# Experts' weights loaded as pairs of chunks into fixed places, with ACT and DVE held to the program's order, in a two-block transformer kernel

## The chip, the cores and the metric

One core of a Trainium2 chip runs the whole program. The metric is the device time of one execution in microseconds (us). Engines: PE multiplies matrices (PEld is its weight load), DVE, ACT and POOL work elementwise, SP issues the loads.

## The reference

All is float32 on 256 tokens of width 1024. The first block holds a retention layer, a dense gated layer, a band-attention layer and a mixture of experts; the second holds two hybrid layers and their MLPs. What the change touches is the mixture of experts:

```
def swiglu(x, w_gate, w_up, w_down):
    return (jax.nn.silu(x @ w_gate) * (x @ w_up)) @ w_down

def moe_swiglu(xn, w_router, w_gate, w_up, w_down):
    logits = (xn @ w_router).astype(jnp.float32)
    top_v, top_i = lax.top_k(logits, TOP_K)
    top_w = jax.nn.softmax(top_v, axis=-1)
    gates = jnp.sum(jax.nn.one_hot(top_i, N_EXPERTS, dtype=jnp.float32) * top_w[..., None], axis=-2)
    gates = gates.astype(xn.dtype)
    y = jnp.zeros_like(xn)
    for e in range(N_EXPERTS):
        y = y + gates[..., e:e + 1] * swiglu(xn, w_gate[e], w_up[e], w_down[e])
    return y
```

Each expert has an inner width of 3584, so its three matrices are 14 x 3 MB of float32.

## The kernel before

**Split products.** PE multiplies in a shorter float format (fp32r). So each float32 operand is split into a high part (ACT copies it into that format) and a low part (DVE subtracts the high part from the original), and a product is three matmuls: high by high, low by high, high by low (`mm3`, L341).

**The stream of weights.** The weights lie in DRAM in the order of use, packed by `packed` (L168) into chunks of 1 MB, 128 partitions by 2048 floats. `Stream` (L228) moves them. `fill` (L256) issues a load on SP's queue into a buffer `wraw` as soon as a pool has a free one: 4 in the pool "raw", and from the attention layer until the last expert's last chunk 3 and 4 more (`widen`, L249), 11 MB in all. `_split` (L277) splits a chunk as two parts of 128x1024: ACT writes `whi` (L288), DVE `wlo` (L289). The last expert's parts are split as two halves of 128x512. `get` (L297) hands the parts to the matmuls and keeps the splits 5 parts ahead, as many as the pool of split parts has buffers.

**The experts.** `experts` (L997) takes the eight experts in turn. Five are *wide* (first, third, fourth, sixth, seventh): room for 128 tokens, three matmuls a product. Three are *narrow* (second, fifth, eighth): room for 64 tokens, whose high and low halves lie side by side, two matmuls a product. An expert has 14 steps. A step has the up product (two chunks, so four parts, here called A, B, C, D; 24 matmuls of 128x512 wide, 16 narrow) and the down product of the step before (one chunk, parts E and F; 12 or 8 matmuls). A prime marks a part of the next step, two primes of the one after that. What is between them:

- wide: sg (ACT's Silu L1031, DVE's product L1032), two transposes on PE (tp, L1038), and the split of tp into hh (ACT, L348) and hl (DVE, L349), which the down product reads;
- narrow: cp (ACT copies the sums, L1043), the fold on PE (tp, L1048, which transposes and adds the halves; 4 matmuls, 8 passes in the trace), sgn (ACT L1052, DVE L1053), and the split of sgn into the two halves of hh (ACT L348, DVE L349).

At the end of an expert the result goes through yh and yl to the tokens' places (L1091, L1093), and for the next pair of experts the tokens are gathered (L956). The `tc.If(most > P)` branch at the end of `moe_layer` doesn't run on these inputs.

**What sets the order.** The program issues instructions in the order of the Python code; the framework's scheduler then orders each engine's instructions by priority and its own estimate of when operands are ready, and each engine works through its list in that order, waiting at semaphores. In the code, `split()` of a step is called after `w.get` of the next step's first up chunk, so after all splits that this call makes.

Of the kernel before, what the change touches and what calls it, by code (L numbers as in the profile page):

```python
# [11 lines left out]
F32 = mybir.dt.float32  # L12
# [3 lines left out]
AF = mybir.ActivationFunctionType  # L16
ALU = mybir.AluOpType
# [150 lines left out]
def packed(plan, arrays):  # L168
    offs, total = offsets(plan)
    out = np.empty(max(total, 1), np.float32)  # L170
    for c, o in zip(plan, offs):
        dst = out[o:o + P * c.kt * c.n].reshape(P, c.kt, c.n)
# [55 lines left out]
class Stream:  # L228


    def __init__(self, prog, plans, raw_bufs, hl_bufs, raw_pool, hl_pool):
        self.nc = prog.nc
        self.items, self.parts, self.first = [], [], []
        for ap, plan in plans:
            offs, _ = offsets(plan)
            for c, o in zip(plan, offs):
                self.first.append(len(self.parts))
                step = max(c.kt // 2, 1)
                self.parts += [(len(self.items), k, step) for k in range(0, c.kt, step)]
                self.items.append((ap, c, o))  # L240
        self.expert = prog.expert
        self.first.append(len(self.parts))
        self.free = {raw_pool: raw_bufs}
        self.base, self.extra = raw_pool, []
# [4 lines left out]
    def widen(self, pool, bufs, until):  # L249

        self.extra.append(pool)
        self.free[pool] = bufs
        self.last = next(i for i, it in enumerate(self.items) if it[1].key == until)
        self.fill()

    def fill(self, most=None):  # L256
        while self.n_raw < min(len(self.items), most or len(self.items)):
            pool = next((p for p in self.extra if self.n_raw <= self.last and self.free[p]), self.base)
            if not self.free[pool]:
                return  # L260
            ap, c, o = self.items[self.n_raw]
            f = c.kt * c.n
            t = pool.tile([P, 2048], F32, name="wraw")
            if c.key[0] in ("eu", "ed"):
                e = self.expert[c.key[1]] if c.key[1] else 0
                src = ap[e:e + 1] if isinstance(e, int) else ap[bass.ds(e, 1)]
                self.nc.sync.dma_start(t[:, :f], src[:, o:o + P * f].rearrange("o (p f) -> (o p) f", p=P))
            else:
                step = f if self.n_raw else f // 2
                for c0 in range(0, f, step):  # L270
                    self.nc.sync.dma_start(t[:, c0:c0 + step],
                                           bass.AP(tensor=ap.tensor, offset=ap.offset + o + c0, ap=[[f, P], [1, step]]))
            self.free[pool] -= 1
            self.raw[self.n_raw] = t, pool
            self.n_raw += 1

    def _split(self):  # L277
        i, k, nk = self.parts[self.n_hl]
        c = self.items[i][1]
        self.fill()  # L280
        t, pool = self.raw[i]
        f = nk * c.n
        hi, lo = (self.hl_pool.tile([P, 1024], F32R, name=n) for n in ("whi", "wlo"))
        n = 1 if c.key[0] in ("eu", "ed") and c.key[1] < NE - 1 else 2
        for i0 in range(0, f, f // n):
            h, l = (x[:, i0:i0 + f // n] for x in (hi, lo))
            src = t[:, k * c.n + i0:k * c.n + i0 + f // n]
            self.nc.scalar.activation(h, src, AF.Copy)  # L288
            self.nc.vector.tensor_tensor(l, src, h.bitcast(F32), op=ALU.subtract)  # L289
        if k + nk == c.kt:  # L290
            self.free[pool] += 1
            del self.raw[i]
        self.hl[self.n_hl] = [x[:, :f].rearrange("p (k n) -> p k n", n=c.n) for x in (hi, lo)]
        self.n_hl += 1
        self.fill()

    def get(self, *keys):  # L297

        at = self.first[self.n_get]
        for key in keys:  # L300
            assert self.items[self.n_get][1].key == key, (self.items[self.n_get][1].key, key)
            self.n_get += 1
        end = self.first[self.n_get]
        while self.n_hl < min(max(end, at + self.hl_bufs), len(self.parts)):
            self._split()
        return [[x[:, k, :] for x in self.hl[i]] for i in range(at, end) for k in range(self.parts[i][2])]


class Program:
    RAW, HL = 4, 5  # L310

    def __init__(self, tc, io, stop=None, dump=None):
        self.tc, self.nc, self.io = tc, tc.nc, io
        self.stop, self.dump_ap = stop, dump
        self.fence, self.in_set = [], []
        self.turns = {}
        self.expert = {}
# [28 lines left out]

    def split_psum(self, hi, lo, ps):
        self.nc.scalar.activation(hi, ps, AF.Copy)  # L348
        self.nc.vector.tensor_tensor(lo, ps, hi.bitcast(F32), op=ALU.subtract)  # L349

# [137 lines left out]
    def run(self):  # L488
        nc, io = self.nc, self.io
        self.we = io["we"].rearrange("(e f) -> e f", e=NE)  # L490
        with ExitStack() as st, ExitStack() as self.later, \
                ExitStack() as self.routed, ExitStack() as self.wide:
            pool = self.lasting = lambda *a, **kw: st.enter_context(self.pool(*a, **kw))
            raw_pool, hl_pool = pool("raw", self.RAW), pool("hl", self.HL)
            self.keep, self.gains = pool("keep", 1), pool("gains", 1)
# [285 lines left out]

    def widen(self, name, bufs):

        self.w.widen(self.wide.enter_context(self.pool(name, bufs)), bufs, ("ed", NE - 1, FFE // 256 - 1))

    def attention_layer(self):
# [3 lines left out]
        with self.pool("bando", side="right") as outs, ExitStack() as mid, ExitStack() as first:  # L790
# [206 lines left out]
    def experts(self, px, pool, gates, slot, w, first, wide):  # L997
# [5 lines left out]
        for e in range(NE):  # L1003
# [21 lines left out]
            def turned(j, ps):  # L1025
# [3 lines left out]
                if wide[e]:  # L1029
                    sg = self.work.tile([P, 256], F32, name="sg", tag="xs", bufs=3)  # L1030
                    nc.scalar.activation(sg, ps[:, :256], AF.Silu)  # L1031
                    nc.vector.tensor_tensor(sg, sg, ps[:, 256:], op=ALU.mult)  # L1032
                    hT[j] = (hh, pool.tile([P, 2, P], F32R, name="hl", bufs=2))

                    def turn():
                        tp = self.bank("tp")
                        for k in range(2):
                            nc.tensor.transpose(tp[:, k * P:(k + 1) * P], sg[:, k * P:(k + 1) * P], self.ident)  # L1038
                        return lambda: self.split_psum(*hT[j], tp[:, :256].rearrange("p (k s) -> p k s", k=2))
# [3 lines left out]
                nc.scalar.activation(cp, ps, AF.Copy)  # L1043

                def turn():
# [3 lines left out]

                    def split():  # L1050
                        sg = self.work.tile([P, 2, 64], F32, name="sgn", tag="xs", bufs=3)
                        nc.scalar.activation(sg, tp[:, :2], AF.Silu)  # L1052
                        nc.vector.tensor_tensor(sg, sg, tp[:, 2:], op=ALU.mult)  # L1053
                        self.split_psum(hh[:, :, :64], hh[:, :, 64:], sg)
                    return split
                return turn

            split = None
            for j in range(nj):
                ps = self.bank("mm")  # L1060
                for k0 in (0, 4):
                    wu = w.get(("eu", e, j, k0 * P))
                    if split:
                        split()
                        split = None
                    for k in range(4):
# [3 lines left out]
                if j == nj - 1:  # L1070
# [4 lines left out]
                    down(rows[:2])  # L1075
                    turn()()
                    down(rows[2:], True)
                else:
                    turn = turned(j, ps)
                    down(rows)  # L1080
                    split = turn()
            with self.tc.high_priority(offset=300) if e == NE - 1 else nullcontext():
# [12 lines left out]
    def moe_layer(self):  # L1095
        nc, tc, io = self.nc, self.tc, self.io
        with self.pool("moex") as px, self.pool("moe") as pool:
            with self.banks(acc="67", mm="45", tp="01", ps="23"):
# [14 lines left out]
                self.experts(px, pool, gates, slot, self.w, first, WIDE)  # L1113
        self.wide.close()
        with tc.If(most > P):
            with self.pool("moe2") as pool, self.pool("raw2", 2) as raw, \
# [4 lines left out]
                self.experts(pool, pool, gates, slot, again, self.gather(pool, pool, slot, GROUPS[0], wide), wide)  # L1121
        self.routed.close()
        return self.at("e")
# [488 lines left out]
```

## Time and profile before

| what | us |
|---|---|
| runs before | 2430.64, 2432.98, 2434.96; median 2432.98 |
| the profiled execution's own time | 2430.28 |
| its span | 2428.5 |
| PE busy | 2369.9 (98 %) |
| DVE busy | 1892.6 (78 %) |
| ACT busy | 1567.7 (65 %) |
| wlo on DVE (L289), 1656 instructions | 1383.4 |
| whi on ACT (L288), 1656 instructions | 1204.1 |
| expert stage, from the first expert's first product to the last's end | 568 to 1532 |

The span runs from the first to the last instruction; the execution's own time has a little around it. "Busy" counts an engine's instructions, not its waits; matmuls are pipelined, so that one shows 0.39 us while the next starts 0.23 us after it. The eight experts begin at about 568, 694, 805, 935, 1056, 1174, 1293 and 1420 us. Of the 606 MB that the program loads, 336 loads of 1 MB are the experts'; in the expert stage the 16 DMA engines are 83 to 97 % busy by expert, against 30 to 70 % in most of the rest. A row of waits names an engine and line, what it waited for, the total, the count and the longest. In a timeline, `x4` is four instructions one behind the other under one start and one duration, and the bracket at a row's end is the engine's idle time before it with what ended it.

### The profile page before, as it was taken

The numbers are of one execution on the slowest core, as the hardware profiler recorded it, in microseconds if no ns is written. First come the engines' busy times: TensorE is split into PE (matmuls) and PEld (weight loads), VectorE is DVE, ScalarE is ACT, GpSimd is POOL, SyncE is SP. The second block draws the span as 40 slices with busy tenths as digits, with TensorE's granted clock in tenths as the row PEclk, the third lists the DMA queues.
The fourth block names the chain that finished last, engine by engine and source line by source line (L and its number), as shares of the span: only waits on it lengthen the run. The fifth ranks groups of instructions, "written<-read, shape, count | busy, mean of one in ns | idle before, by whom it ended". The sixth has DMA issues, their size and how long they took to land. (4 is left out here: it accounts for less than half of the span.)

```text
span 2428.5 us, 35659 instructions
## 1 busy us (share of the span) xinstructions
PE 2369.9 (98%) x13032; PEld 1972.4 (81%) x13032; DVE 1892.6 (78%) x3026; ACT 1567.7 (65%) x2609; POOL 61.1 (3%) x105
## 2 busy tenths in 40 slices
PE   8999999999999999999999999899999999999999
PEld 6978998887876787876788876698789989878998
DVE  6756567778999889899998899878776567877655
ACT  6446555667888777778777789645755554575554
POOL 0000000000000000000000000100000000100000
PEclk9999999999999999999999999999999999999999
DMA  7445555567989998999999999534345554434553
GB/s 286 167 174 208 191 191 191 194 247 265 369 333 394 360 359 335 359 356 409 356 369 343 364 356 393 148 132 161 133 167 199 189 173 139 170 126 177 194 189 107
DMA packets 88393, 605.72 MB, mean 249 GB/s; under 512 B 10480, under 2 KB 12144, under 8 KB 17296
## 3 DMA queue, kind: packets, MB, share of 16 engines
q1 hardware_dynamic: 85792, 593.91, 65.4%
q0 software_dynamic: 2416, 9.44, 1.7%
q8 instruction: 104, 1.70, 0.3%
q14 instruction: 81, 0.66, 0.1%
HBM read 602.26 MB, written 1.05 MB: 248 GB/s over the span
## 5 line engine op out<-in xcount | busy, mean ns | idle before, releaser
L289 DVE TENSOR_TENSOR wlo<-wraw,whi 128x512 fp32r<-128x512 f32 (+1 forms) x1656 | 1383.4, 876 | 369.4 <-ACT whi L288 356.1
L288 ACT ACTIVATE whi<-wraw 128x512 fp32r<-128x512 f32 (+1 forms) x1656 | 1204.1, 776 | 438.9 <-PE mm L344 201.9
L343 PE MATMUL mm<-xth,whi 128*128 128x256 f32 x1296 | 366.3, 283 | 0.0
L345 PE MATMUL mm<-xth,wlo 128*128 128x256 f32 x1296 | 364.0, 281 | 1.2 <-DVE wlo L289 1.2
L344 PE MATMUL mm<-xtl,whi 128*128 128x256 f32 x1296 | 364.2, 281 | 0.0
L345 PEld LDWEIGHTS mm<-xth,wlo 128*128 128x128 f32 x1296 | 247.1, 191 | 2.1 <-DVE wlo L289 1.4
L343 PEld LDWEIGHTS mm<-xth,whi 128*128 128x128 f32 x1296 | 243.6, 188 | 4.9 <-issue 3.0
L344 PEld LDWEIGHTS mm<-xtl,whi 128*128 128x128 f32 x1296 | 243.8, 188 | 3.7 <-issue 2.1
L344 PE MATMUL acc<-wlo,hh 128*128 128x512 f32 x624 | 243.6, 390 | 0.0
L345 PE MATMUL acc<-whi,hl 128*128 128x512 f32 x624 | 243.5, 391 | 0.0
L343 PE MATMUL acc<-whi,hh 128*128 128x512 f32 x624 | 231.6, 391 | 1.5 <-ACT hh L348 1.5
L343 PE MATMUL mm<-whi,xth 128*128 128x512 f32 (+2 forms) x592 | 231.7, 391 | 0.6 <-ACT whi L288 0.4
L344 PE MATMUL mm<-wlo,xth 128*128 128x512 f32 (+2 forms) x592 | 231.5, 391 | 0.3 <-DVE wlo L289 0.3
L345 PE MATMUL mm<-whi,xtl 128*128 128x512 f32 (+2 forms) x592 | 229.5, 388 | 0.5 <-DVE xtl L349 0.5
L343 PE MATMUL mm<-whi,xgh 128*128 128x512 f32 x560 | 226.2, 404 | 2.6 <-ACT whi L288 2.6
L344 PE MATMUL mm<-wlo,xgh 128*128 128x512 f32 x560 | 223.8, 400 | 3.0 <-DVE wlo L289 3.0
L345 PE MATMUL mm<-whi,xgl 128*128 128x512 f32 x560 | 222.2, 397 | 0.0
L1013 PE MATMUL mm<-wlo,xgh 128*128 128x512 f32 x336 | 143.2, 426 | 5.2 <-DVE wlo L289 4.4
L343 PEld LDWEIGHTS acc<-whi,hh 128*128 128x128 f32 x624 | 117.1, 188 | 26.4 <-ACT hh L348 3.3
L345 PEld LDWEIGHTS acc<-whi,hl 128*128 128x128 f32 x624 | 117.1, 188 | 25.0 <-DVE hl L349 0.6
L344 PEld LDWEIGHTS acc<-wlo,hh 128*128 128x128 f32 x624 | 117.2, 188 | 23.4 <-DVE wlo L289 0.3
L1012 PE MATMUL mm<-whi,xgh 128*128 128x512 f32 x336 | 134.4, 400 | 0.0
(386 smaller groups left out, 3091.7 us busy)
## 6 DMA issues: line engine op xcount, KB each, us to landing
wraw<-in_we_dram SPq DMA_DIRECT2D x336, 1024.0 KB, 5.8
wraw<-in_w_dram SPq DMA_DIRECT2D x218, 1024.0 KB, 4.8
wraw<-in_w_dram SPq DMA_DIRECT2D x4, 912.0 KB, 4.7
wraw<-in_w_dram SPq DMA_DIRECT2D x6, 512.0 KB, 3.6
bias<-in_rel_rows_dram POOLq DMA_DIRECT2D x4, 768.0 KB, 4.6
gain<-in_norm_ffn_dram POOLq DMA_DIRECT2D x2, 512.0 KB, 6.6
gn<-in_ret_gn_dram SPq DMA_DIRECT2D x4, 256.0 KB, 3.2
gain<-in_norm_ple_dram POOLq DMA_DIRECT2D x2, 512.0 KB, 6.6
```

What stands on the lines that cost most here:

```text
L288: self.nc.scalar.activation(h, src, AF.Copy)
L289: self.nc.vector.tensor_tensor(l, src, h.bitcast(F32), op=ALU.subtract)
L343: mm(out, l[0], r[0], start=start, stop=False)
L344: mm(out, l[0], r[1], start=False, stop=False)
L345: mm(out, l[1], r[0], start=False, stop=stop)
L1012: nc.tensor.matmul(out, x[0], wk[0], start=start, stop=False)
L1013: nc.tensor.matmul(out, x[0], wk[1], start=False, stop=stop)
```

## The change

1. `packed` lays two neighbouring chunks of an expert side by side for each partition, and `fill` loads such a pair with one DMA of 2 MB into two neighbouring places of a fixed tile. The places are tiles of 4, 2 and 4 chunks (10 MB) in the place of pools of 4, 3 and 4 buffers (11 MB). A place is free when both its parts are split; a pair is loaded when two neighbouring places are free.
2. `inorder` chains instructions of ACT, and of DVE, so that the scheduler keeps them in the program's order: the experts' whi and wlo, sg, cp, sgn, hh and hl.
3. `get` takes steps to put `between` its splits: hh and hl of a wide step stand behind the first split that the call makes; of a narrow step, sgn behind the first and hh behind the second.

```diff
 def packed(plan, arrays):
...
+        if c.key[0] in ("eu", "ed"):
+            o -= half * P * c.kt * c.n
+            dst = out[o:o + 2 * P * c.kt * c.n].reshape(P, 2, c.kt, c.n)[:, half]
+            half = 1 - half
...
+    def room(self, pool, n, last):
+        t = pool.tile([P, n, 2048], F32, name="wraw")
+        self.last[id(t)] = last
+        self.free += [(t, k) for k in range(n)]
...
     def fill(self, most=None):
         while self.n_raw < min(len(self.items), most or len(self.items)):
-            pool = next((p for p in self.extra if self.n_raw <= self.last and self.free[p]), self.base)
-            if not self.free[pool]:
+            ap, c, o, n = self.items[self.n_raw]
+            free = [p for p in self.free if self.n_raw < self.last[id(p[0])]]
+            size = 1
+            if n is not None and self.pairs:
+                assert n % 2 == 0
+                size = 2
+                free = [(t, k) for t, k in free if k % 2 == 0 and (t, k + 1) in self.free]
+            if not free:
                 return
...
-                self.nc.sync.dma_start(t[:, :f], src[:, o:o + P * f].rearrange("o (p f) -> (o p) f", p=P))
+                src = src[:, n // 2 * 2 * P * f:(n // 2 + 1) * 2 * P * f].rearrange("o (p k f) -> (o p) k f", p=P, k=2)
+                self.nc.sync.dma_start(t[:, k:k + size], src[:, n % 2:n % 2 + size])
...
     def _split(self):
...
-            self.nc.scalar.activation(h, src, AF.Copy)
-            self.nc.vector.tensor_tensor(l, src, h.bitcast(F32), op=ALU.subtract)
+            act = self.nc.scalar.activation(h, src, AF.Copy)
+            dve = self.nc.vector.tensor_tensor(l, src, h.bitcast(F32), op=ALU.subtract)
+            if c.key[0] in ("eu", "ed"):
+                self.prog.inorder(act=act, dve=dve)
...
-    def get(self, *keys):
+    def get(self, *keys, between=()):
...
         while self.n_hl < min(max(end, at + self.hl_bufs), len(self.parts)):
             self._split()
+            if between:
+                between.pop(0)()
+        for step in between:
+            step()
...
+    def inorder(self, **ins):
+        for e, i in ins.items():
+            self.after(i, [self.line[e]] if e in self.line else [])
+            self.line[e] = i
...
-            self.widen("raw3", 3)
+            self.widen("raw3", 2)
...
             for j in range(nj):
                 ps = self.bank("mm")
                 for k0 in (0, 4):
-                    wu = w.get(("eu", e, j, k0 * P))
-                    if split:
-                        split()
-                        split = None
+                    wu = w.get(("eu", e, j, k0 * P), between=steps)
+                    steps = []
```

The rest of the diff passes `sg`, `cp`, `sgn`, `hh` and `hl` through `inorder` and returns the steps of `turn` as a list. `self.after` adds an order without a semaphore. Outside the expert stage every engine's instructions stay in their order.

How the order moves in three places (L1066, L1078, L1088, L307, L375 and L1073 of the change are L1031, L1043, L1052, L288, L348 and L1038 of before). ACT, a step in the middle of the third expert (wide), before:

```order
L1031 ACTIVATE sg<-mm 128x256
L288 ACTIVATE whi<-wraw 128x1024 x2
L348 ACTIVATE hh<-tp 128x256
L288 ACTIVATE whi<-wraw 128x1024 x4
L1031 ACTIVATE sg<-mm 128x256
```

and of the change:

```order
L1066 ACTIVATE sg<-mm 128x256
L307 ACTIVATE whi<-wraw 128x1024
L375 ACTIVATE hh<-tp 128x256
L307 ACTIVATE whi<-wraw 128x1024 x5
L1066 ACTIVATE sg<-mm 128x256
```

hh has moved ahead of one split; five splits stand behind it, not four. PE in the same expert where the transposes (tp) of a step in the middle stand, before, with the tiles' numbers (acc are the down product's sums, mm the next up product's):

```order
L344 MATMUL acc_8210<-wlo_8916,hh_8870 128x512
L345 MATMUL acc_8210<-whi_8915,hl_8874 128x512
L1038 MATMUL tp_8964<-ident_83,sg_8948 128x128 x2
L343 MATMUL mm_8967<-whi_8921,xgh_7106 128x512
L344 MATMUL mm_8967<-wlo_8922,xgh_7106 128x512
```

and of the change, a step in the middle of the same expert:

```order
L371 MATMUL mm_8695<-wlo_8667,xgh_6943 128x512
L372 MATMUL mm_8695<-whi_8666,xgl_6944 128x512
L370 MATMUL mm_8695<-whi_8671,xgh_6943 128x512
L371 MATMUL mm_8695<-wlo_8672,xgh_6943 128x512
L372 MATMUL mm_8695<-whi_8671,xgl_6944 128x512
L1073 MATMUL tp_8692<-ident_84,sg_8676 128x128 x2
L370 MATMUL mm_8695<-whi_8671,xgh_6943 128x512
L371 MATMUL mm_8695<-wlo_8672,xgh_6943 128x512
```

The transposes stood right behind the down matmuls; they now stand behind 15 of the next step's 24 up matmuls (part whi_8671 is the third of its four), in the next step behind 13, and so on by turns. ACT, a step in the middle of the fifth expert (narrow), before:

```order
L1043 ACTIVATE cp<-mm 128x512
L288 ACTIVATE whi<-wraw 128x1024 x2
L1052 ACTIVATE sgn<-tp 128x128
L288 ACTIVATE whi<-wraw 128x1024 x2
L348 ACTIVATE hh<-sgn 128x2x64
L288 ACTIVATE whi<-wraw 128x1024 x2
L1043 ACTIVATE cp<-mm 128x512
```

and of the change:

```order
L1078 ACTIVATE cp<-mm 128x512
L307 ACTIVATE whi<-wraw 128x1024
L1088 ACTIVATE sgn<-tp 128x128
L307 ACTIVATE whi<-wraw 128x1024
L375 ACTIVATE hh<-sgn 128x2x64
L307 ACTIVATE whi<-wraw 128x1024 x4
L1078 ACTIVATE cp<-mm 128x512
```

sgn and hh stand one split earlier each, four splits follow. On PE the fold, which stood between the down matmuls, now stands behind 9 and 6 by turns of the next step's 16 up matmuls (in the last expert behind 11 and 10).

## Rows read from the trace of the kernel before

**Rows 1.** Windows, fifth expert: us; PE, PEld, DVE, ACT, POOL busy; clock; DMA share; GB/s.
```profile
1056.00:1174.00 118.00, 111.48 (x508) 80.18 (x507) 113.21 (x128) 101.50 (x137) 0.00 (x0) 1.00 0.97 387
```

**Rows 2.** Waits of ACT in the expert stage, 568 to 1540 us: total, times, longest.
```profile
ACT whi L288 <- DMA wraw<-in_we_dram: 7.8, 23, 0.8
```

**Rows 3.** Waits of SP's queue, 607 to 1500 us: total, times, longest.
```profile
SPq L267 <- DVE wlo L289: 466.1, 201, 6.6
```

**Rows 4.** The experts' loads as one tile: from issue to landing.
```profile
DMA to landing us min/median/max: 4.6/5.8/11.7
```

**Rows 5.** Timeline of PE in a wide step: start, duration, instruction, idle before.
```profile
975.85 0.38 PE L1038 MATMUL tp<-ident,sg 128*128 128x128 f32 x2
...
976.30 0.39 PE L344 MATMUL mm<-wlo,xgh 128*128 128x512 f32 x1
...
981.42 0.40 PE L345 MATMUL mm<-whi,xgl 128*128 128x512 f32 x1
...
984.38 0.38 PE L1038 MATMUL tp<-ident,sg 128*128 128x128 f32 x2
```

**Rows 6.** Timeline of ACT in the same wide step.
```profile
976.26 0.39 ACT L348 ACTIVATE hh<-tp 128x256 fp32r<-128x256 f32 x1 [0.66 <-PE tp L1038]
976.61 3.90 ACT L288 ACTIVATE whi<-wraw 128x1024 fp32r<-128x1024 f32 x4
```

**Rows 7.** Timeline of DVE in the same wide step.
```profile
977.70 4.63 DVE L289 TENSOR_TENSOR wlo<-wraw,whi 128x1024 fp32r<-128x1024 f32 x4 [0.32 <-ACT whi L288]
```

**Rows 8.** Timeline of ACT in a narrow step of the fifth expert.
```profile
1089.02 0.28 ACT L1052 ACTIVATE sgn<-tp 128x128 f32<-128x128 f32 x1 [0.36 <-PE tp L1048]
1089.19 2.00 ACT L288 ACTIVATE whi<-wraw 128x1024 fp32r<-128x1024 f32 x2
...
1096.56 0.28 ACT L1052 ACTIVATE sgn<-tp 128x128 f32<-128x128 f32 x1 [0.37 <-PE tp L1048]
```

**Rows 9.** Timeline of DVE in the same narrow step.
```profile
1092.55 0.28 DVE L349 TENSOR_TENSOR hh<-sgn,hh 128x128 fp32r<-128x128 f32 x1
1092.75 2.35 DVE L289 TENSOR_TENSOR wlo<-wraw,whi 128x1024 fp32r<-128x1024 f32 x2
```

**Rows 10.** Timeline of PE in the last expert.
```profile
1471.79 1.00 PE L1048 MATMUL tp<-fold,cp 128*128 128x64 f32 x8
```

**Rows 11.** Timeline of ACT in the last expert.
```profile
1461.60 0.61 ACT L288 ACTIVATE whi<-wraw 128x512 fp32r<-128x512 f32 x1
...
1465.21 0.28 ACT L1052 ACTIVATE sgn<-tp 128x128 f32<-128x128 f32 x1 [0.18 <-PE tp L1048]
...
1472.83 0.28 ACT L1052 ACTIVATE sgn<-tp 128x128 f32<-128x128 f32 x1 [0.18 <-PE tp L1048]
```

**Rows 12.** Timeline of DVE in the last expert.
```profile
1466.89 2.50 DVE L289 TENSOR_TENSOR wlo<-wraw,whi 128x512 fp32r<-128x512 f32 x4
...
1469.50 4.91 DVE L289 TENSOR_TENSOR wlo<-wraw,whi 128x512 fp32r<-128x512 f32 x8
```

**Rows 13.** Timeline of ACT, early steps of the second expert (narrow).
```profile
704.07 0.58 ACT L1043 ACTIVATE cp<-mm 128x512 f32<-128x512 f32 x1
...
766.91 0.60 ACT L1043 ACTIVATE cp<-mm 128x512 f32<-128x512 f32 x1 [0.84 <-PE mm L1013]
```

**Rows 14.** Timeline of ACT, first step of the fifth expert.
```profile
1070.21 0.60 ACT L1043 ACTIVATE cp<-mm 128x512 f32<-128x512 f32 x1 [1.99 <-PE mm L1013]
...
1078.69 0.60 ACT L1043 ACTIVATE cp<-mm 128x512 f32<-128x512 f32 x1 [1.18 <-PE mm L1013]
```

**Rows 15.** Waits of PE where the second expert ends, 798 to 808 us.
```profile
PE mm L343 <- ACT whi L288: 1.3, 1, 1.3
PE mm L344 <- DVE wlo L289: 0.8, 1, 0.8
```

**Rows 16.** Busy time and granted clock there.
```profile
804.00:806.00 2.00, 2.00 (x6) 1.57 (x5) 1.53 (x2) 0.60 (x1) 0.00 (x0) 0.50 1.02 430
```

**Rows 17.** Waits of PE where the fifth expert ends, 1163 to 1180 us.
```profile
PE mm L343 <- ACT whi L288: 1.2, 1, 1.2
```

More of the change, by code (lines that the diff above doesn't have):

```diff
@@ L170, in packed @@
     out = np.empty(max(total, 1), np.float32)
+    half = 0
     for c, o in zip(plan, offs):
-        dst = out[o:o + P * c.kt * c.n].reshape(P, c.kt, c.n)
+        if c.key[0] in ("eu", "ed"):
+            o -= half * P * c.kt * c.n
+            dst = out[o:o + 2 * P * c.kt * c.n].reshape(P, 2, c.kt, c.n)[:, half]
+            half = 1 - half
+        else:
+            dst = out[o:o + P * c.kt * c.n].reshape(P, c.kt, c.n)
         at = 0
@@ L239, in __init__ @@
                 self.parts += [(len(self.items), k, step) for k in range(0, c.kt, step)]
-                self.items.append((ap, c, o))
+                self.items.append((ap, c, o, plan.index(c) if c.key[0] in ("eu", "ed") else None))
         self.expert = prog.expert
         self.first.append(len(self.parts))
-        self.free = {raw_pool: raw_bufs}
-        self.base, self.extra = raw_pool, []
+        self.free, self.last = [], {}
+        self.room(raw_pool, raw_bufs, len(self.items))
         self.hl_pool, self.hl_bufs = hl_pool, hl_bufs
@@ L247, in __init__, with widen @@
         self.n_raw = self.n_hl = self.n_get = 0
[L249 to L253, printed above, removed]
+    def room(self, pool, n, last):
+        t = pool.tile([P, n, 2048], F32, name="wraw")
+        self.last[id(t)] = last
+        self.free += [(t, k) for k in range(n)]
+    def widen(self, pool, n, until):
+        self.room(pool, n, 1 + next(i for i, it in enumerate(self.items) if it[1].key == until))
         self.fill()
@@ L270, in fill @@
                 for c0 in range(0, f, step):
-                    self.nc.sync.dma_start(t[:, c0:c0 + step],
+                    self.nc.sync.dma_start(t[:, k, c0:c0 + step],
                                            bass.AP(tensor=ap.tensor, offset=ap.offset + o + c0, ap=[[f, P], [1, step]]))
-            self.free[pool] -= 1
-            self.raw[self.n_raw] = t, pool
-            self.n_raw += 1
+            for i in range(size):
+                self.free.remove((t, k + i))
+                self.raw[self.n_raw] = t, k + i
+                self.n_raw += 1
     def _split(self):
@@ L295, in _split @@
         self.fill()
-    def get(self, *keys):
+    def get(self, *keys, between=()):
+        between = list(between)
         at = self.first[self.n_get]
@@ L315, in __init__ @@
         self.fence, self.in_set = [], []
-        self.turns = {}
+        self.turns, self.line = {}, {}
         self.expert = {}
@@ L780, in softmax_pair, with widen @@
         self.split_psum(*out, po[:, :T])
-    def widen(self, name, bufs):
-        self.w.widen(self.wide.enter_context(self.pool(name, bufs)), bufs, ("ed", NE - 1, FFE // 256 - 1))
+    def widen(self, name, n):
+        self.w.widen(self.wide.enter_context(self.pool(name)), n, ("ed", NE - 1, FFE // 256 - 1))
     def attention_layer(self):
@@ L1048, in turn, with silu @@
                         nc.tensor.matmul(tp[:, c], cp[:, c * P:(c + 1) * P], self.fold, start=True, stop=True)
[L1050 to L1055, printed above, removed]
+                    sg = self.work.tile([P, 2, 64], F32, name="sgn", tag="xs", bufs=3)
+                    def silu():
+                        self.inorder(act=nc.scalar.activation(sg, tp[:, :2], AF.Silu),
+                                     dve=nc.vector.tensor_tensor(sg, sg, tp[:, 2:], op=ALU.mult))
+                    return [silu, lambda: self.split_psum(hh[:, :, :64], hh[:, :, 64:], sg, True)]
                 return turn
-            split = None
+            steps = []
             for j in range(nj):
@@ L1061, in experts @@
                 for k0 in (0, 4):
-                    wu = w.get(("eu", e, j, k0 * P))
-                    if split:
-                        split()
-                        split = None
+                    wu = w.get(("eu", e, j, k0 * P), between=steps)
+                    steps = []
                     for k in range(4):
@@ L1075, in experts @@
                     down(rows[:2])
-                    turn()()
+                    for step in turn():
+                        step()
                     down(rows[2:], True)
@@ L1080, in experts @@
                     down(rows)
-                    split = turn()
+                    steps = turn()
             with self.tc.high_priority(offset=300) if e == NE - 1 else nullcontext():
@@ L1114, in moe_layer @@
         self.wide.close()
+        self.line = {}
         with tc.If(most > P):
-            with self.pool("moe2") as pool, self.pool("raw2", 2) as raw, \
+            with self.pool("moe2") as pool, self.pool("raw2") as raw, \
                     self.pool("hl2", 4) as hl, self.banks(acc="67", mm="45", tp="01", ps="23"):
```

32 lines of the change are left out of this document (17 added, 15 removed).

## The prediction, made before the change was run

> **What bounds the kernel now.** I went first to the waits of the loads, since the change is named after them. SP's queue waits mostly for DVE's wlo [rows 3]: a load goes out when its place has been split, not when the memory is ready. ACT, the first reader of a load, waited for one 23 times in the whole expert stage, 7.8 us together [rows 2]. So loads do not bound it, and 7.8 us is the most that faster ones could give.
>
> Then the windows and timelines, step by step. In a **wide** expert PE is the bound: from transpose to transpose 8.53 us [rows 5], the matmuls one behind the other at 0.23 us (22 from 976.30 to 981.42). In a **narrow** one DVE is: it is busy 113.21 of 118 us [rows 1], and a step lasts 7.54 us (sgn at 1089.02, then 1096.56) [rows 8]. In the last expert, whose splits are halves, it lasts 7.62 us (1465.21 to 1472.83) [rows 11]. ACT has idle time in both, but it is in the middle of every chain: what stands behind what on ACT decides when a part is split.
>
> **The change, part by part.** *Loads.* 336 loads of 1 MB become 168 of 2 MB; a pair waits until both its places are split, and there are 10 places, not 11. SP issues nothing else in this stage, so nothing is queued behind that longer wait. Cover: 10 places hold 20 parts, and DVE splits one per 1.14 us at best (four in 4.63 us [rows 7], two in 2.35 [rows 9]). A pair issued as soon as its places are free is needed about 8 chunks, 16 parts or 18 us, later; the longest landing of 1 MB was 11.7 us and the median 5.8 [rows 4]. I cost it at nothing. Bounds: 7.8 us gained if every one of those waits [rows 2] goes; as much lost if they double.
>
> *Order in a wide step.* ACT used to split two parts between sg and hh, now one (D'), so hh stands earlier on it; the next part E' comes behind hh. But PE's transposes, which hh waits for, stood right behind the down matmuls, and now stand behind 15 and 13 of the next step's 24 up matmuls by turns. From the transposes' start on: hh starts 0.41 later (975.85 to 976.26), E' on ACT 0.35 behind it [rows 6]. One whi is 1.05 (four take 3.90 [rows 6], two 2.00 [rows 8]); DVE starts 0.04 behind its end (977.70 [rows 7]), and one wlo is 1.21. With 0.05 to PE (an estimate, after that 0.04) E' can be used at 0.41 + 0.35 + 1.05 + 0.04 + 1.21 + 0.05 = 3.11 us. PE wants it after 0.22 of transposes (975.85 to 976.30, less one matmul), the rest of the 24 up matmuls and two that need only whi: behind 15, at 0.22 + 11 x 0.23 = 2.75, so it stands 0.36 us; behind 14, 0.13; behind 13 or fewer it finds E' ready. In the third, fourth, sixth and seventh expert I count 16 steps with 15 and 5 with 14: 16 x 0.36 + 5 x 0.13 = **6.4 us lost**, on PE, which is the bound there. In the first expert the transposes stand behind 11 or fewer: nothing.
>
> *Order in a narrow step.* The eight passes of the fold used to lie inside the down matmuls, now behind 9 and 6 of the next 16 up matmuls by turns. From the fold's start: sgn 1.04 later (1471.79 [rows 10] to 1472.83 [rows 11]), E' on ACT 0.17 on [rows 8], 1.05 for it and 0.04: wlo of E' starts at 2.30. Then DVE runs without a gap: E' 1.14, hh 0.20 (1092.55 to 1092.75 [rows 9]), F' and A'' 1.14 each, B'' 1.21, and 0.05 to PE: 7.18. The next fold stands one matmul behind that (6) or four (9): 7.41 or 8.10 us after the last, against 7.54. Over the second and fifth expert there are nine with 9, ten with 6 and one with 7 (7.64): 9 x 0.56 - 10 x 0.13 + 0.10 = **3.8 us lost**.
>
> *Last expert.* The same with halves (whi 0.61 [rows 11], wlo 0.60 apart and 0.69 long, from four in 2.50 and eight in 4.91 [rows 12]): 1.04 + 0.17 + 0.61 + 0.04 to E', then 1.20 + 0.20 + 3 x 1.20 + 0.69 + 0.05 to the first half of C'', 7.60. The folds stand behind 10 and 11, five each: 7.83 and 8.06 against 7.62. 5 x 0.21 + 5 x 0.44 = **3.2 us lost**.
>
> *What goes.* Early in the second expert hh stood too late on ACT: eight steps took 62.84 us (704.07 to 766.91) [rows 13], not 8 x 7.54; in the new order hh stands behind one split: 2.5 us. The fifth expert's first step took 8.48 [rows 14]: 0.9 us. At the second expert's end PE waited 1.3 and 0.8 us for the next expert's first part [rows 15] and right after it ran 2 us at a granted clock of 0.50, its lower level of 1.2 GHz [rows 16], behind those gaps: 3.1 us with the 1.0 us that this cost. At the fifth expert's end it waited 1.2 us [rows 17] and once more 0.8 us, as in [rows 15]: 2.0 us. In the new order that first part is split ahead of the last step's work. **8.5 us gained.**
>
> *Unknown.* At each expert's end sgn (or sg) and hh of the last step now stand side by side on ACT with no split between them, so ACT stands while PE and DVE go to and fro. PE has 5 up matmuls there and the down matmuls of the step before, so I take 0. Bounds: 0, and the 2.1 us of [rows 15] at seven ends, 15 us. The hand-over to PE, taken as 0.05, lies between 0 and the 0.18 us that ACT stood between the fold's end and sgn [rows 11]: over the 40 late steps (21 wide, 9 narrow, 10 in the last expert) -2 to +5 us. Of the gains, a third of the 2.5 and of each end's wait may stay: 3 us less gain, or as much more where the lower clock cost more than I count.
>
> *Sum.* 6.4 + 3.8 + 3.2 - 8.5 = 4.9 us slower than the profiled execution's 2430.28, 2435.2; the median of the runs shown lies 2.7 us above that execution, so I add 4.9 to the median: **2438 us**.
>
> **Pages against rows.** The Trainium skill ("DMA: Bandwidth & Descriptors", Bandwidth) measured 341 GB/s for a load of 1 MB and 425 for one of 16 MB, so it would have these loads gain from doubling. Here the fifth expert as a whole moved 387 GB/s with 1 MB loads, so the trace differs, and by the rule the sum would fall by the 7.8 us at most.
>
> The Trainium skill ("Perfetto Trace Analysis", Optimization Strategy) says that a gap repeating on the engine that should be saturated can mean too little room for the next tile. That speaks against giving up a megabyte; by it 7.8 us more would be lost. The waits that the loads cause here are the 7.8 us of ACT, so I keep my sum.
>
> **The rivals.**
> - *A, the forecast, 0.48:* the loops as worked. Its own range, 2433 to 2446, is 2438 with the hand-overs (-2 to +5) and the gains (3 either way). For it: the order is fixed, every duration has a row. Against: gains and losses are both some ten us, and the difference is small.
> - *B, they cancel, 0.12:* each loop 0.14 us shorter than worked (hh lasts 0.39 and the next whi starts 0.35 on [rows 6]; every link may overlap a little like that), 35 steps (16 wide, 9 narrow, 10 last) x 0.14 = 4.9: 2433.
> - *C, faster, 0.20:* the late transposes cost nothing. It turns on one point: when PE comes to the down matmuls of a wide step, is E' split? If hh and E' together are 0.36 us quicker than their rows, it is, and a narrow loop that is as much shorter stays within 7.54 on the mean. Then only the gains stand: 2433 - 8.5 = 2424. For it: ACT's idle time before hh is then longer, and no buffer is waited for. Against: each link has its row from the same operations.
> - *D, slower, 0.13:* ACT stands at the ends, 2.1 us at seven of them on top of A: 2453. For it: such a wait with the clock behind it is in the trace. Against: what PE has to do there.
> - *E, the loads decide, 0.07:* 2 MB loads take the 7.8 us of waits [rows 2] away: 2438 - 7.8 = 2430. It decides if each of those waits reaches PE. Against: those waits are 0.8 us at most and ACT has idle time to take them up. (The Trainium skill's Bandwidth section, above, speaks for this one.)
> That the edit does nothing is excluded: the order of ACT, DVE and PE is another one.
>
> **How the numbers follow.** A measurement of this kernel can tell 0.2 %, 4.9 us. A lies at that edge: of its 0.48 I give 0.30 to slower and 0.18 to no change. With D, slower is 0.43; with B and E, no change is 0.37; C is faster, 0.20. The range goes to C and D with a little around them, 2421 to 2453; the likeliest case alone is 2433 to 2446.
>
> **What would show it.** In the profile after: PE waiting 0.3 to 0.4 us for wlo of the down part in every second wide step, sg's starts by turns longer and shorter than 8.53; narrow steps by turns near 7.4 and 8.1, the last expert 7.8 to 8.1; ACT's wait for the transposes growing from 0.66 us by about 3 in wide steps; no gap and no lower clock at 802 to 807 us; 168 loads that land later with ACT's waits for them as small. The forecast is wrong if PE's waits for E' are missing (C), if the ends of the experts are longer than before (D), or if ACT waits for loads by tens of us.

## The result and the profile after

The changed kernel takes **2449.81 us** (median of 4 runs, 2448.70 to 2450.33) against 2432.83 us beside it: ratio 1.007, 95 % interval 1.0057 to 1.0082. It is slower by 17 us, clear of the 4.9 us that a measurement can tell. That is inside the range of 2421 to 2453; the forecast of 2438 had the sign right and a third of the size. The time lies above the forecast's own range of 2433 to 2446, and the wider one holds it because it reaches to rival D.

The span went from 2428.5 to 2446.9 us, 18.4 more. Where it came from can be read step by step: the start of sg (wide) or cp (narrow) on ACT marks each of the 8 x 14 steps. Differences of those starts, after less before:

| piece | forecast | measured |
|---|---|---|
| first expert, its first step and steps 2 to 13 | 0 | +2.0 (start -1.1, first step +2.0, the rest +1.0) |
| third, fourth, sixth, seventh expert (wide), steps 2 to 13 | +6.4 | +10.6 (3.6, 1.6, 1.7, 3.7) |
| second and fifth expert (narrow), steps 2 to 13 | +0.4 | +3.2 (-0.3, +3.6) |
| last expert, steps 2 to 13 | +3.2 | +4.5 |
| the seven ends with the next expert's first step | -5.1 | -0.9 |
| behind the last expert's last cp (2.9 more at the branch among it) | 0 | -0.9 |

(The narrow forecast is 3.8 less the 2.5 and 0.9 of early steps; the rows above add up to 4.9 and 18.4.)

A wide step, from the timeline of the profile after, in the fourth expert; ACT first (start, duration, instruction, idle before it):

```profile
1019.63 0.36 ACT L1066 ACTIVATE sg<-mm 128x256 f32<-128x256 f32 x1
...
1023.62 0.38 ACT L375 ACTIVATE hh<-tp 128x256 fp32r<-128x256 f32 x1 [2.68 <-PE tp L1073]
1023.90 4.84 ACT L307 ACTIVATE whi<-wraw 128x1024 fp32r<-128x1024 f32 x5
1028.65 0.37 ACT L1066 ACTIVATE sg<-mm 128x256 f32<-128x256 f32 x1
...
1032.11 0.38 ACT L375 ACTIVATE hh<-tp 128x256 fp32r<-128x256 f32 x1 [2.15 <-PE tp L1073]
```

then DVE, PE's weight loads and PE in the same step:

```profile
1024.99 5.77 DVE L308 TENSOR_TENSOR wlo<-wraw,whi 128x1024 fp32r<-128x1024 f32 x5 [0.52 <-ACT whi L307]
```
```profile
1026.27 0.19 PEld L371 LDWEIGHTS acc<-wlo,hh 128*128 128x128 f32 x1 [0.56 <-DVE wlo L308]
```
```profile
1023.21 0.38 PE L1073 MATMUL tp<-ident,sg 128*128 128x128 f32 x2
...
1025.52 0.62 PE L370 MATMUL acc<-whi,hh 128*128 128x512 f32 x2
1026.27 0.50 PE L371 MATMUL acc<-wlo,hh 128*128 128x512 f32 x1
1026.61 0.40 PE L372 MATMUL acc<-whi,hl 128*128 128x512 f32 x1
```

This is the chain of the forecast, link by link. The transposes start at 1023.21 and hh 0.41 later; ACT had stood 2.68 us for them, where it stood 0.66 before [rows 6]: 2.0 more, not the 3 of the forecast. The first of the five splits behind hh is E'; its wlo starts 1.78 us after the transposes (1.85 forecast) and ends at 1026.21, and the matmul that needs it starts 0.06 later. PE had come there at 1025.98 (two matmuls after 1025.52) and stood 0.29 us. Then the first matmul behind the gap lasts 0.50 and the next starts 0.34 later, not 0.23: a stall costs 0.11 more than its wait. So a stall is 0.40 (0.36 forecast). By turns the steps take 9.03 and 8.49 us (1019.63 to 1028.65 is the long one).

A narrow step of the fifth expert, ACT and DVE, then PE:

```profile
1116.20 0.28 ACT L1088 ACTIVATE sgn<-tp 128x128 f32<-128x128 f32 x1 [0.89 <-PE tp L1083]
...
1124.42 0.28 ACT L1088 ACTIVATE sgn<-tp 128x128 f32<-128x128 f32 x1 [1.57 <-PE tp L1083]
```
```profile
1117.46 1.23 DVE L308 TENSOR_TENSOR wlo<-wraw,whi 128x1024 fp32r<-128x1024 f32 x1 [0.23 <-ACT whi L307]
1118.60 0.28 DVE L376 TENSOR_TENSOR hh<-sgn,hh 128x128 fp32r<-128x128 f32 x1
1118.80 5.76 DVE L308 TENSOR_TENSOR wlo<-wraw,whi 128x1024 fp32r<-128x1024 f32 x5
```
```profile
1115.16 1.00 PE L1083 MATMUL tp<-fold,cp 128*128 128x64 f32 x8
...
1122.35 0.50 PE L1048 MATMUL mm<-wlo,xgh 128*128 128x512 f32 x1
1122.68 0.39 PE L1047 MATMUL mm<-whi,xgh 128*128 128x512 f32 x1
...
1123.38 1.00 PE L1083 MATMUL tp<-fold,cp 128*128 128x64 f32 x8
```
```profile
1122.35 0.19 PEld L1048 LDWEIGHTS mm<-wlo,xgh 128*128 128x128 f32 x1 [0.38 <-DVE wlo L308]
```

The fold of 1115.16 has its sgn 1.04 later and wlo of E' at 2.30, as forecast. The wait that ends last ahead of the next fold is the one for wlo of B'': PE gets it at 1122.35, 7.19 us after the fold (7.18 forecast). But the matmul there lasts 0.50, and the next starts 0.33 later and not 0.23, so the next fold comes 8.22 us after this one (8.10 forecast). sgn now waits 0.89 and 1.57 us by turns, 0.36 before [rows 8]. On the way PE also waits for hh, 41 times and 32.2 us in the whole stage, against 8 times and 11.0 us before:

```profile
PE acc L1047 <- DVE hh L376: 32.2, 41, 2.1
```

Where the second expert ends, PE now waits 0.4 and 0.4 us where it waited 1.3 and 0.8 [rows 15], and the granted clock, 0.50 before [rows 16], is full:

```profile
PE mm L371 <- DVE wlo L308: 0.4, 1, 0.4
PE mm L370 <- ACT whi L307: 0.4, 1, 0.4
```
```profile
804.00:806.00 2.00, 2.00 (x10) 1.62 (x9) 2.00 (x3) 2.00 (x4) 0.00 (x0) 1.00 1.03 434
```

Where the fifth expert ends, the waits of PE have not gone (1163 to 1200 us; before 1.2 [rows 17] and 0.8):

```profile
PE mm L371 <- DVE wlo L308: 1.2, 2, 0.7
PE acc L1047 <- DVE hh L376: 0.8, 2, 0.4
PE ps L1012 <- DVE xgl L376: 0.8, 1, 0.8
```

In the last step of the third expert, which gathers tokens (`xgh`), ACT took sg ahead of the last gathers before (their first came 2.7 us behind it), and takes it behind them after:

```profile
924.79 0.39 ACT L1031 ACTIVATE sg<-mm 128x256 f32<-128x256 f32 x1
```
```profile
927.80 0.49 ACT L1020 ACTIVATE xgh<-ps 128x384 fp32r<-128x384 f32 x1 [1.81 <-PE ps L1012]
...
929.50 0.39 ACT L1066 ACTIVATE sg<-mm 128x256 f32<-128x256 f32 x1
```

The loads land later, as 2 MB, and ACT waits for none in the stage (7.8 us before [rows 2]):

```profile
L285 SPq DMA_DIRECT2D wraw<-in_we_dram x168: 327/333/428, 511.7 to 1516.5; - x168
...
DMA to landing us min/median/max: 7.5/9.8/12.8
```

### The profile page after: what moved, and what is told of

It reads as the page before. It is cut to its first block, busy times and chain, and to the rows that moved or that the text cites. A ratio compares the mean times of both kernels' runs of the same rounds, so it can differ in the third digit from the quotient of the medians.

```text
span 2446.9 us, 34846 instructions
## 1 busy us (share of the span) xinstructions
PE 2368.3 (97%) x13032; PEld 1969.9 (81%) x13032; DVE 1888.8 (77%) x3026; ACT 1551.0 (63%) x2609; POOL 61.2 (3%) x105
## 3 DMA queue, kind: packets, MB, share of 16 engines
q0 software_dynamic: 2416, 9.44, 1.7%
## 5 line engine op out<-in xcount | busy, mean ns | idle before, releaser
L307 ACT ACTIVATE whi<-wraw 128x512 fp32r<-128x512 f32 (+1 forms) x1656 | 1197.3, 774 | 406.0 <-PE mm L371 200.0
```

Of the source, the lines that this page charges most:

```text
L307: act = self.nc.scalar.activation(h, src, AF.Copy)
```

## The experiments

Theory: the loss comes round the hand-off. PE's transposes or fold stand late, ACT in its fixed order waits for them with hh, and the splits behind hh come late to PE. First rival: the loads (pairs land later, a megabyte less). Second rival: holding ACT and DVE in order costs by itself. "Before" beside the first four was 2429.20 us.

**order_only**: the change without its part 1, so with `packed`, `fill`, `widen` and the pools of the kernel before. The lines that tell most, against the changed kernel:

```diff
-                self.nc.sync.dma_start(t[:, k:k + size], src[:, n % 2:n % 2 + size])
+                self.nc.sync.dma_start(t[:, :f], src[:, o:o + P * f].rearrange("o (p f) -> (o p) f", p=P))
...
-            self.widen("raw3", 2)
+            self.widen("raw3", 3)
```

> The loads of before (1 MB each, 11 MB of buffers), with the change's order of ACT and DVE. Theory (the hand-off: hh and the splits behind it wait on ACT for transposes or a fold that stand late on PE): the loss stays although the loads are those of before. On PE the transposes stand behind 15 up matmuls in nearly every steady wide step (after: 15 and 13 by turns) and the fold behind 9 in nearly every step of the fifth expert (after: 9 and 6), so these steps take about 9.0 and 8.2 us each, not by turns, and the whole is slower than the change, 2452 to 2465 us. Rival (the loads: pairs land later, one megabyte less): about 2433, as before.

Measured: 2459.41 us, ratio 1.0119 (1.0102 to 1.0135). The loads of before don't take the loss away, they make it larger, as the orders said: steady wide steps 8.95 to 8.99 us, the fifth expert 8.21 in nearly every step. The loss of the change is not one of its loads.

**pairs_only**: part 1 alone.

```diff
     def inorder(self, **ins):
-        for e, i in ins.items():
...
+        return
...
-                    wu = w.get(("eu", e, j, k0 * P), between=steps)
+                    wu = w.get(("eu", e, j, k0 * P))
+                    for step in steps:
+                        step()
```

> The change's loads (2 MB pairs, 10 MB) without the chains of order and with the steps after the call's splits, as before. The scheduler puts the transposes behind 0 or 7 up matmuls and the fold into the down matmuls. Theory (hand-off): no late transposes, so near before, 2428 to 2440. Rival (loads): the loss stays, about 2450, and ACT's waits for loads are tens of us.

Measured: 2480.27 us, ratio 1.0207 (1.0190 to 1.0224): both expectations miss, by 40 and 30 us. ACT waits for no load. The wide steady steps are 8.56 us; the narrow ones take 10.45 and 7.37 by turns. The timeline of ACT and of DVE in the fifth expert:

```profile
1138.27 3.89 ACT L307 ACTIVATE whi<-wraw 128x1024 fp32r<-128x1024 f32 x4
1142.07 0.26 ACT L1086 ACTIVATE sgn<-tp 128x128 f32<-128x128 f32 x1
1144.22 0.31 ACT L375 ACTIVATE hh<-sgn 128x128 fp32r<-128x128 f32 x1 [1.89 <-DVE sgn L1087]
```
```profile
1139.35 4.63 DVE L308 TENSOR_TENSOR wlo<-wraw,whi 128x1024 fp32r<-128x1024 f32 x4 [0.62 <-ACT whi L307]
1143.90 0.28 DVE L1087 TENSOR_TENSOR sgn<-sgn,tp 128x128 f32<-128x128 f32 x1
```

The scheduler, free to choose, orders the narrow steps otherwise when the loads are pairs: four splits ahead of sgn, so that hh waits 1.89 us behind four wlo. (That it is the scheduler's own estimate of the loads which moves it, I only argue.) So the pairs cost 51 us through the order that they bring about, and parts 2 and 3 of the change take back 30 to 34 of these (30 between the two medians, 34 with each beside its own "before").

**pe_hold**: the change, with the transposes or fold held directly behind the down matmuls.

```diff
+                        if j and held:
+                            self.after(head, held)
+                            held.clear()
```

(`held` are the step's transposes or fold, `head` the next up product's first matmul.)

> The change, and besides the first up matmul of a step is ordered behind the transposes (or fold) of the step before, so that these stand directly behind the down matmuls on PE. Theory (hand-off): the loops close in time, wide steps 8.53 to 8.57 us, narrow ones about 7.5, last expert about 7.6; the 19 us that the steps lost are back, and the late hh of the second expert's early steps is gone too: 2425 to 2433. Rival (loads): still about 2450. Rival (ACT and DVE kept in order cost by themselves): steps stay longer than before without a wait for the transposes, over 2440.

Measured: 2442.32 us, ratio 1.005 (1.0033 to 1.0067): the time misses the theory and is what the second rival said. The narrow half came out better than said, 7.29 us in every steady step of the second and fifth expert and 7.63 in the last: there the theory holds. The wide half missed: 8.77 in every step, without turns. And the first steps of the fourth, sixth and seventh expert grew to between 11.5 and 12.2 us (8.7 to 9.5 in the change), where PE waits 1.5 to 4.3 us for sg with the up product held behind it. I put the 8.77 down to the way round with five splits between hh and sg.

**hh_later**: the change, with each step one split later (in narrow experts the call makes two splits, so sgn and hh both come behind the second).

```diff
-                        return [lambda: self.split_psum(*hT[j], tp[:, :256].rearrange("p (k s) -> p k s", k=2), True)]
+                        return [lambda: None, lambda: self.split_psum(*hT[j], tp[:, :256].rearrange("p (k s) -> p k s", k=2), True)]
...
-                    return [silu, lambda: self.split_psum(hh[:, :, :64], hh[:, :, 64:], sg, True)]
+                    return [lambda: None, silu, lambda: None, lambda: self.split_psum(hh[:, :, :64], hh[:, :, 64:], sg, True)]
```

> The change with the steps between the splits one split later: ACT does sg, two splits, hh, four splits, kept in that order; PE's transposes still stand late (behind 13 and 14 up matmuls). Theory (hand-off): E' is then split ahead of hh and only F' behind it, which PE wants 1.4 us later, so the late transposes cost nothing in wide steps (8.53 to 8.6) and little in narrow ones: 2428 to 2438. If late transposes cost time wherever hh stands, about 2450; loads: about 2450.

Measured: 2459.27 us, ratio 1.012 (1.0103 to 1.0137), slower than all that was expected. Here too the two halves part. Wide steps are 9.03 and 8.07 by turns, 8.55 on the mean, as before: with E' split ahead of hh the late transposes cost nothing. The narrow ones went to 8.42, since sgn and hh now stand side by side on ACT, and DVE's part of sgn behind two wlo:

```profile
1104.38 2.00 ACT L307 ACTIVATE whi<-wraw 128x1024 fp32r<-128x1024 f32 x2
1106.28 0.26 ACT L1088 ACTIVATE sgn<-tp 128x128 f32<-128x128 f32 x1
1108.32 0.31 ACT L375 ACTIVATE hh<-sgn 128x128 fp32r<-128x128 f32 x1 [1.78 <-DVE sgn L1089]
```

**best**, **best_1mb**, **best_full**: the hold from the second step on, hh behind two splits in wide experts alone; the second with the loads of before; the third with the last expert in whole parts. Against the change, the first two pieces in all three, the last in the third alone:

```diff
+                        if j and held:
+                            if j > 1:
+                                self.after(head, held)
+                            held.clear()
...
-                        return [lambda: self.split_psum(*hT[j], tp[:, :256].rearrange("p (k s) -> p k s", k=2), True)]
+                        return [lambda: None, lambda: self.split_psum(*hT[j], tp[:, :256].rearrange("p (k s) -> p k s", k=2), True)]
...
-        n = 1 if c.key[0] in ("eu", "ed") and c.key[1] < NE - 1 else 2
+        n = 1 if c.key[0] in ("eu", "ed") else 2
```

> The change's loads and chains of order, with two edits: PE's transposes (or fold) are ordered ahead of the next step's up matmuls from the second step on, and in the wide experts hh stands behind two splits, not one (narrow ones as in the change). Theory (hand-off; a step is as long as the longest way round from transposes to transposes): wide steps 8.53 to 8.57 us, since four splits stand between hh and sg and not five; narrow ones 7.29; last expert 7.63. Against before, steps 2 to 13 lose some 12 us together, the ends are as in the change: 2416 to 2424 us beside a before of 2429. Rival (the pairs and the smaller room cost something that only shows now): PE or ACT waits for loads and the time is 2430 or more.

> The same orders with the loads of before (1 MB each, 11 MB of buffers). Theory (loads are no bound in either form): the same within 3 us as with pairs. Rival (pairs land later and hold two places): faster than with pairs by over 5 us. Rival (larger loads are more efficient): slower than with pairs by over 5 us.

> As the first, and the last expert is split in whole parts, not halves. Theory (DVE bounds a narrow step, and a whole wlo costs 1.14 us per part where two halves cost 1.20): the last expert's 12 steady steps take 7.29 and not 7.63 us, 4 us less in all, if the chain from fold to fold stays under that. Rival: the longer splits make the fold's chain the bound, no gain.

Measured beside 2431.38: 2434.25 us, ratio 1.0015 (1.0006 to 1.0024); 2429.99, 0.9995 (0.9986 to 1.0004); 2427.23, 0.9986 (0.9977 to 0.9995). The first missed, and not as its rival said, since ACT waits for no load: the narrow steps are 7.29, but the wide ones stayed at 8.77, with one split less between hh and sg, so my reason for 8.77 was wrong. PE's weight loads, DVE and ACT in the fourth expert of the first one show the right one:

```profile
991.61 0.20 PEld L1074 LDWEIGHTS tp<-ident,sg 128*128 128x128 f32 x2 [0.41 <-DVE sg L1068]
```
```profile
990.00 1.23 DVE L308 TENSOR_TENSOR wlo<-wraw,whi 128x1024 fp32r<-128x1024 f32 x1 [0.17 <-ACT whi L307]
991.14 0.41 DVE L1068 TENSOR_TENSOR sg<-sg,mm 128x256 f32<-128x256 f32 x1
```
```profile
988.91 1.06 ACT L307 ACTIVATE whi<-wraw 128x1024 fp32r<-128x1024 f32 x1 [0.34 <-PE mm L372]
```

The transposes wait for sg, not for a split. sg on DVE stands behind a wlo in the program's order (a split of the down chunk's `get`), and the whi before that waits for a buffer which PE frees with the end of the same up product. From there to the transposes it is a split on ACT, one on DVE and sg, longer than the 12 down matmuls beside it. The last expert's steps fell from 7.63 to 7.29 us in whole parts, as said; the whole fell by 7.0 us, 4 of them by these steps.

Nearly the same orders with pairs cost 4.3 us more than with 1 MB loads (in the two traces 9 of some 990 instructions of ACT and 11 of DVE stand otherwise); that is between what the theory and its rival said. Part of it stands where the program branches behind the last expert. ACT's wait there is 4.9 us in the kernel before, 7.8 in the one after, 9.0 and 5.1 in this pair, and 6.2 to 9.0 in every kernel with pairs against 4.4 to 5.2 in every one with 1 MB. The row of the profile after, and of before:

```profile
ACT junk L406 <- DVEq L1150: 7.8, 1, 7.8
```
```profile
ACT junk L371 <- DVEq L1115: 4.9, 1, 4.9
```

Behind the experts' loads SP issues the next layer's, five up to 1531.0 us in the kernel before and six up to 1554.5 in the one after. So before, SP comes to the branch at 1531.0, ahead of ACT (1534.7), and is through at 1536.5; after, it comes at 1554.6, behind ACT (1550.9), and is through at 1560.2, and DVE with it. SP stays there 5.2 to 5.9 us in all of these kernels, with pairs or without. What differs is when it comes: 1.2 to 3.7 us ahead of ACT in every kernel with 1 MB loads, and as much behind ACT in every one with pairs. What it stays for (the landing of its last load is likely) was not tried by itself.

**sg_first**, **sg_first_1mb**: as best_full, but in wide experts sg stands ahead of the down chunk's splits (and hh behind three splits); the second with the loads of before.

```diff
+                early = wide[e] and 0 < j < nj - 1
+                turn = turned(j, ps) if early else None
                 rows = rows_of(j - 1) if 0 < j < nj - 1 else []
...
-                    turn = turned(j, ps)
+                    turn = turn or turned(j, ps)
```

> As the one before (pairs, orders held, transposes ahead of the next up product, last expert in whole parts), but in the wide experts sg stands ahead of the two splits of the down chunk, and hh behind three splits: ACT does sg, three splits, hh, three splits. The wide steps of 8.77 us were not long because of the number of splits between hh and sg, as I had said: in the trace PE waits 0.2 us for sg, which on DVE stands behind a wlo whose buffer PE only frees with the end of the same up product. Theory (that wait): with sg ahead of it the wide steps take 8.53 to 8.57 us, 0.21 x 12 x 5 = 13 us less: 2413 to 2418 us beside a before of 2430. Rival (the wide step is long because all is held in order, or the five buffers bind it): still 8.77 and 2427.

> The same orders with the loads of before (1 MB each, 11 MB of buffers). What the pairs cost in the pair of kernels before this was 4 us, of which 2 to 3 lie where the program branches behind the last expert (a load that goes out late there must land first), and the rest in the first steps of an expert. If so: 2 to 5 us faster than with pairs. If the pairs cost nothing: within 2 us.

Measured beside 2429.36: 2417.55 us, ratio 0.9947 (0.9933 to 0.9960), and 2413.92, 0.9932 (0.9918 to 0.9946). The wide steps are 8.56, so the wait for sg was the reason: what is held in order did cost by itself in *pe_hold*, at this one place. The timeline of the first of them in the fourth expert, ACT and DVE:

```profile
975.35 0.38 ACT L1067 ACTIVATE sg<-mm 128x256 f32<-128x256 f32 x1 [1.73 <-PE mm L372]
975.63 2.94 ACT L307 ACTIVATE whi<-wraw 128x1024 fp32r<-128x1024 f32 x3
978.47 0.37 ACT L376 ACTIVATE hh<-tp 128x256 fp32r<-128x256 f32 x1
978.74 2.05 ACT L307 ACTIVATE whi<-wraw 128x1024 fp32r<-128x1024 f32 x2
```
```profile
975.76 0.42 DVE L1068 TENSOR_TENSOR sg<-sg,mm 128x256 f32<-128x256 f32 x1 [0.38 <-ACT sg L1067]
```

sg follows the up product at once, and hh finds its transposes ready. The pairs cost 3.6 us here (2 to 5 expected). Both kernels beat before and after; the faster one keeps the loads of before.

## Why the prediction was right and where it was not

**Right: the mechanism and the sign.** Of the terms that it summed, the wide stall measures 0.40 us for 0.36, the narrow way round 8.22 for 8.10, the last expert's 8.20 and 7.97 for 8.06 and 7.83; the narrow half of pe_hold and the wide half of hh_later take the cost away by moving the hand-off, and order_only keeps it with the other loads. Rivals B and C fall with that: the links are as long as their rows. Rival E falls as well: ACT's waits for loads went from 7.8 us to none and no gain shows; in best_1mb they are 14.6 us, and that kernel is 4.3 us faster than best, which has none. Rival D's price was too high, but its sign came in part: four of the seven ends are longer than before, by less than 2.1 us each.

**Wrong: the size, 11.8 us too small** (13.5 between the profiled executions, which the pieces add up to), in four terms of the sum.
- *The narrow steps (3.8 less 3.4 us forecast, 3.2 measured).* I let a step with 6 be 0.13 shorter than 7.54. It takes 7.53, and one with 9 takes 8.22: each stall leaves 0.11 us of slower starts behind it, on both turns. I had no term for it, though matmuls of 0.50 behind a gap stand in narrow steps of before as well. In the last expert it is the 0.14 a step too. And the fifth expert's last step, which gathers tokens, takes 10.34 us for 8.64: 1.7 of the 2.8 that the forecast lacks, also without a term. Early steps of 7.29 give some back.
- *The wide steps (6.4 forecast, 10.6 measured).* The fourth and sixth expert are as forecast, 1.6 and 1.7 for 1.6 each, in part by luck: 1.1 and 1.3 are the turns, the rest is one step of 9.73 or 9.44 less shorter ones from 8.08 on, which I did not have. The third and seventh, which gather the next experts' tokens, lose 3.6 and 3.7: the third's last step takes 12.1 us (9.2 before), the seventh's last two 9.8 and 9.9 (8.7 and 8.8), and in the third sg now stands on ACT behind the gather's xgh. Of that I had no term; part of it returns at the third's end (-2.0).
- *The ends (5.1 us gained forecast, 0.9 measured).* The second and fifth expert's ends gained 1.4 and 0.9 us, not 3.1 and 2.0. At the second the low clock went as said and PE's waits shrank from 2.1 to 0.8 us; at the fifth the waits did not go. The ends of the first, fourth, sixth and seventh, where nothing was to be gained, lost 0.7 to 1.0 each. So "I take 0" for sgn and hh side by side was the wrong choice within its bounds of 0 and 15. At the first three ends ACT now stands 0.4 to 2.3 us ahead of the last step's hh and 2.3 to 3.4 ahead of the next one's, against 0 to 1.3 and 0 to 1.6 before; that this is what costs it is not shown, since no run changed the ends alone.
- *The first expert (0 forecast, 2.0 measured):* its first step and the one that gathers.

Of the loads, too, a premise failed: "SP issues nothing else in this stage" leaves out the next layer's loads, which stand behind the last pairs. They bring SP late to the branch, where ACT waits 2.9 us more. In the table other gains cover it (last row, -0.9).

And one thing the sum could not show, as it compared the order before with the order after. The loads cost nothing by waiting, as said, but the pairs alone would have cost 51 us through the scheduler's order. So I never saw that the chains undo most of what the pairs do.

The Trainium skill ("DMA: Bandwidth & Descriptors", Bandwidth) measured more GB/s for a load of 16 MB than for one of 1 MB. Here a pair lands in 9.8 us at the median and one load in 5.8 [rows 4], less than twice, which points the same way, though with other loads in flight; the time did not gain, and ACT waited for no load. The Trainium skill ("VectorE: DVE Perf Modes", The TRN2 errata) says that a fixed cost comes with every instruction of VectorE and ScalarE that reads SBUF, so a large tile pays once and pieces pay each. The trace agrees: the last expert's steps are 7.63 us with two halves a part and 7.29 with one whole.

## What to carry to other kernels

Where an engine is held to a fixed order, read the way round from each hand-off back to itself, over all engines, with the place of PE's part as the scheduler set it: the longest of these ways is the step, and an instruction waits for all that stands ahead of it, also for a buffer that the consumer frees late. Who fixes the order on some engines of the way leaves the rest to the scheduler; here ACT and DVE were held and PE was not, and holding PE too paid only when sg had its right place as well (2442 us, then 2418). And when one edit has two parts, look at the order of each alone, since one may undo what the other does.

## What the runs showed of the hardware

- A matmul behind a stall lasts 0.50 us in the record and the next one starts 0.33 or 0.34 us later (1026.27, 1122.35), against 0.39 and 0.23 in a row: a short stall costs PE about 0.11 us beyond the wait itself.
- A pair of 2 MB lands in 9.8 us at the median, 12.8 at most, against 5.8 and 11.7 for 1 MB; with nearly the same orders the pairs cost 3.6 to 4.3 us.
- The waits that the clock went down behind (1.3 and 0.8 us at the second expert's end, granted clock 0.50) shrank to 0.4 and 0.4 us after, and the clock there stayed at 1.00. At the fifth expert's end PE waited 1.2 and 0.8 us before, and the clock stayed at 1.00 there too (1164 to 1176 us).
